# The 8x8 base of the triangular inverses: block doubling from size 1 on TensorE in place of substitution on VectorE

## The chip, the cores and the metric

One NeuronCore of a Trainium2 chip runs the whole program, in one launch. The metric is the device time of one execution in microseconds (us), from the first to the last instruction and what the runtime adds around them. Three runs of the kernel before took 4042.07, 4048.28 and 4054.17 us: a median of 4048.28.

## The reference

Two residual blocks follow each other on 512 tokens of 2048 channels, all in float32. The first has a gated convolution and a differential attention; the change doesn't touch it. The second mixes with two recurrences, each over a context of 256 tokens and then the 512 tokens themselves, in both directions. Both need inverses of unit lower triangular matrices:

```python
def gated_delta_chunked(q, k, v, beta, g, s0):       # chunks of 64 tokens, 8 heads of 128
    ...
    decay = jnp.exp(jnp.where(tril, g[..., :, None] - g[..., None, :], -jnp.inf))
    kb = k * beta[..., None]
    lmat = jnp.where(strict, jnp.einsum('bhncd,bhnsd->bhncs', kb, k) * decay, 0.0)
    tmat = lax.linalg.triangular_solve(eye + lmat, jnp.broadcast_to(eye, lmat.shape),
                                       left_side=True, lower=True, unit_diagonal=True)
    u = tmat @ (v * beta[..., None])
    wk = tmat @ (kb * jnp.exp(g)[..., None])
    ...
def rwkv7_scan(r, w, k, v, kk, b_vec, s0):           # 16 heads of 64, token by token
    def step(state, inp):
        sa = -jnp.einsum('bhvk,bhk->bhv', state, kk_t)
        state = (state * w_t[:, :, None, :] + sa[..., None] * b_t[:, :, None, :]
                 + v_t[..., None] * k_t[:, :, None, :])
        return state, jnp.einsum('bhvk,bhk->bhv', state, r_t)
```

The kernel works the second recurrence in chunks of 64 tokens too, and each chunk then needs the inverse of a unit triangular 64 x 64 matrix as well.

## The kernel before

**The engines.** Large products ("dense" below, L136 in `products`) take weights in blocks of 128 x 128 against 512 tokens (256 for the context), in three passes, since each float32 operand is cut into a high part (ScalarE, L104) and a rest (VectorE, L105, tile `wlo`). The recurrences add many small products on TensorE and elementwise work on VectorE and ScalarE.

**The order.** A scheduler orders each engine's instructions when the program is built, from priorities; every engine then works through its own list in order. Dense products that the recurrences don't wait for (the next heads' inputs, the output's products) stand between the recurrences' small ones, mostly in runs of six (`K.burst`).

**The inverse.** `inv64` (L337 to L405) gets in `nm` the matrices -M^T of `n` tiles, each with two 64 x 64 units on the halves of the partitions, and gives ((I + M)^-1)^T. First comes the base, the inverses of the 8 x 8 blocks on the diagonal, all on VectorE: a mask (L342) and a sum (L344) fetch the blocks, and substitution goes through the columns, six times the three instructions shuffle, product and sum (L351 to L353), each waiting for the one before. Four masked copies (L356) spread the result into 32 x 32 blocks (`iv_u`), and a transpose (L358) gives `iv_t`. Then come doubling levels, here two (8 to 16, 16 to 32): 4 products of 32 x 32 for each of the `n` tiles (L368), a copy by ScalarE (L370), again 4 `n` products (L374), a predicated copy that puts the new blocks into `iv_u` (L376), and a transpose (L377). A last step (L381 to L404) joins 32 to 64.

**How often.** `inv64` is called 56 times: by the gated delta rule (`gdn_core`, tiles `gd_*`) for 8 heads and 2 directions, with n = 2 for the context and n = 4 for the 512 tokens; by the second recurrence (`rwkv_pair`, tiles `rg_*`, two heads at a time) with n = 8, 8 times for the context and 16 times for the tokens. So n = 2, 4 and 8 come 16, 16 and 24 times. One float32 product of 32 x 32 leaves two records in the trace: a level's group of L368 or L374 has 8 n records, so 16, 32 and 64.

## Time and profile before

| | |
|---|---|
| median of 3 runs | 4048.28 us |
| the profiled execution, span | 4056.2 us |
| PE (TensorE products) busy | 3829.7 us, 94% |
| PEld (weight loads) busy | 2916.8 us, 72% |
| DVE (VectorE) busy | 2808.6 us, 69% |
| ACT (ScalarE) busy | 1389.2 us, 34% |
| POOL (GpSimd) busy | 479.8 us, 12% |
| mean granted TensorE clock | 0.964 |

The span goes from the first to the last instruction of the one execution that was profiled; of that execution no other time is given, and its span is 7.9 us above the median of the runs. Busy time is the time in which at least one instruction of the engine was under way; records of neighbouring products overlap, since they are pipelined. A granted clock of 1.00 is 2.4 GHz and 0.50 is 1.2 GHz; the mean of a stretch lies between.

The inverses stand in three stretches of the program: from 600 to 1700 us (the context, n = 2 and then 8, beside the first block's products), from 2400 to 3000 us (gated delta rule on the tokens, n = 4) and from 3000 to 3950 us (second recurrence, n = 8, at its start the last head's with n = 4).

### The profile page before, as it was taken

To read this page: it belongs to the slowest core of one execution; us is meant where nothing else is said; L and a number is where in the kernel's file an instruction comes from. 1 tells how busy PE (TensorE), PEld (TensorE's weight loads), DVE (VectorE), ACT (ScalarE), POOL (GpSimd) and SP (SyncE) were. 2 spreads that over 40 slices of the span, in tenths; PEclk is the share of its full clock that TensorE was granted. 3 is DMA by queue.
4 is the path that set the end of the run, shared out by engine and by line. 5 is a ranking of instruction groups with operands and counts; after the bars stand their busy time and mean duration, and the time that the engine had idled before them with its cause. 6 is when DMAs were issued, how large, how long until landed. Compare 5 with 4: busy or idle time off the path is not lost. (4 is left out here: it accounts for less than half of the span.)

```text
span 4056.2 us, 82730 instructions
## 1 busy us (share of the span) xinstructions
PE 3829.7 (94%) x33202; PEld 2916.8 (72%) x33202; DVE 2808.6 (69%) x7413; ACT 1389.2 (34%) x2825; POOL 479.8 (12%) x572
## 2 busy tenths in 40 slices
PE   8999878999999999999999799999999999999997
PEld 4676668876767767776887477877777777766776
DVE  3366787688777777744532977878667877777766
ACT  3312333323343434322322333333323443434333
POOL 0000221002110100000221301101001110111102
PEclk9999899999999999999999899999999998999998
DMA  8766435433334333424533332222223211222236
GB/s 320 266 212 200 157 127 165 146 113 110 126 114 125 104 104 99 149 91 143 207 113 122 104 96 69 71 72 74 81 84 107 67 64 55 76 67 88 91 120 203
DMA packets 213121, 497.01 MB, mean 123 GB/s; under 512 B 40576, under 2 KB 73600, under 8 KB 212736
## 3 DMA queue, kind: packets, MB, share of 16 engines
q1 hardware_dynamic: 212736, 491.72, 37.0%
q8 instruction: 261, 4.28, 0.4%
q14 instruction: 124, 1.02, 0.1%
HBM read 438.54 MB, written 53.08 MB: 121 GB/s over the span
## 5 line engine op out<-in xcount | busy, mean ns | idle before, releaser
L136 PE MATMUL pd<-big,whi 128*128 128x512 f32 x5344 | 1788.5, 412 | 9.1 <-ACT big L331 8.0
L136 PEld LDWEIGHTS pd<-big,whi 128*128 128x128 f32 x5344 | 965.7, 191 | 262.0 <-issue 27.8
L136 PE MATMUL pd<-big,wlo 128*128 128x512 f32 x2800 | 1114.0, 398 | 3.8 <-DVE wlo L105 3.8
L104 ACT CAST whi<-wraw 128x1024 fp32r<-128x1024 f32 (+2 forms) x500 | 506.7, 1014 | 1109.7 <-PE pd L136 1045.6
L105 DVE TENSOR_TENSOR wlo<-wraw,whi 128x1024 fp32r<-128x1024 f32 (+2 forms) x483 | 579.2, 1199 | 310.8 <-ACT whi L104 276.7
L136 PEld LDWEIGHTS pd<-big,wlo 128*128 128x128 f32 x2800 | 534.8, 191 | 128.0 <-DVE wlo L105 6.4
L136 PE MATMUL pd<-hc,whi 128*128 128x256 f32 x1184 | 236.3, 299 | 17.8 <-ACT gc_up L515 6.0
L136 PEld LDWEIGHTS pd<-hc,whi 128*128 128x128 f32 x1184 | 193.2, 200 | 23.4 <-ACT gc_up L515 6.4
L136 PE MATMUL pd<-hc,wlo 128*128 128x256 f32 x592 | 175.4, 297 | 28.3 <-DVE wlo L105 24.0
L136 PE MATMUL pd<-ext,whi 128*128 128x512 f32 x512 | 184.4, 401 | 3.8 <-DVE ext L105 3.8
L1075 DVE SCALAR_TENSOR_TENSOR cv_y<-cv_up,vec,cv_y 128x512 f32<-128x512 f32 x240 | 179.7, 749 | 4.7
L136 PE MATMUL pd<-fa,whi 128*128 128x512 f32 x448 | 153.1, 423 | 0.3 <-DVE wo L1462 0.2
L136 PEld LDWEIGHTS pd<-hc,wlo 128*128 128x128 f32 x592 | 117.9, 199 | 34.1 <-DVE wlo L105 27.8
L971 ACT ACTIVATE rg_zw<-rg_H,rg_wc 64x64 f32<-64x64 f32 x320 | 104.7, 343 | 47.1 <-DVE rg_H L989 38.7
L858 POOL TENSOR_TENSOR rg_bk<-rg_th,rg_L 64x512 f32<-64x512 f32 x48 | 67.7, 1410 | 425.5 <-ACT rg_L L837 193.0
L989 DVE SCALAR_TENSOR_TENSOR rg_H<-pc,rg_wc,rg_zw 64x64 f32<-64x64 f32 x320 | 90.5, 283 | 38.9 <-PE pc L981 30.5
L136 PEld LDWEIGHTS pd<-ext,whi 128*128 128x128 f32 x512 | 97.2, 190 | 27.8 <-DVE ext L105 4.6
L221 DVE SCALAR_TENSOR_TENSOR ada_ev<-wraw,cs_ada,ada_ev 128x512 f32<-128x512 f32 x120 | 94.8, 790 | 15.8 <-DMA wraw<-in_wada_dram 14.8
L520 DVE SCALAR_TENSOR_TENSOR gc_y<-gc_up,vec,gc_y 128x512 f32<-128x512 f32 (+1 forms) x160 | 103.2, 645 | 2.0
L136 PEld LDWEIGHTS pd<-fa,whi 128*128 128x128 f32 x448 | 82.2, 194 | 20.2 <-issue 1.1
L370 ACT COPY iv_y<-px 128x256 f32<-128x256 f32 (+2 forms) x112 | 33.0, 294 | 177.2 <-PE px L368 176.9
L906 PE MATMUL px<-rg_C,rg_bk 64*128 64x128 f32 x512 | 92.5, 311 | 0.3 <-DVE rg_C L909 0.3
(575 smaller groups left out, 5915.3 us busy)
## 6 DMA issues: line engine op xcount, KB each, us to landing
wraw<-in_w_dram SPq DMA_DIRECT2D x372, 512.0 KB, 3.6
wraw<-in_wada_dram SPq DMA_DIRECT2D x192, 512.0 KB, 4.6
wraw<-in_wo_dram SPq DMA_DIRECT2D x32, 512.0 KB, 3.5
sgl<-sgd SPq DMA_DIRECT2D x48, 256.0 KB, 3.4
wraw<-in_wout_dram SPq DMA_DIRECT2D x20, 512.0 KB, 4.1
wraw<-in_w_dram SPq DMA_DIRECT2D x32, 256.0 KB, 3.9
sgd<-msg SPq DMA_DIRECT2D x32, 256.0 KB, 3.7
wraw<-in_wco_dram SPq DMA_DIRECT2D x16, 512.0 KB, 3.5
```

Source lines behind the costliest of these rows:

```text
L104: K.nc.scalar.copy(hi, src)
L105: (eng or K.nc.vector).tensor_tensor(lo, src, hi.bitcast(F32), op=ALU.subtract)
L136: nc.tensor.matmul(ps[:, :T], lhsT=a[:, k], rhs=b, start=(n == 0), stop=(n == 3 * (k1 - k0) - 1))
L221: nc.vector.scalar_tensor_tensor(ev, raw[:, k], cs[:, kk, 0:1], ev, op0=ALU.mult, op1=ALU.add)
L370: nc.scalar.copy(ys, yp)
L520: nc.vector.scalar_tensor_tensor(y, up[:, t:t + T], w[:, t:t + 1], y, op0=ALU.mult, op1=ALU.add)
L858: nc.gpsimd.tensor_tensor(bk[uq, :, u], th[uq], F[uq], op=mul)
L906: nc.tensor.matmul(pg[:, m], lhsT=bk[q, 4 * r + m].rearrange("p x c -> p (x c)"), rhs=C[q, 4 * r + m, u], start=True, stop=True, tile_posi ...
L971: nc.scalar.activation(zw[hv[u], d], H[hv[u], ms[d], u], AF.Copy, scale=wn[hv[u], 4 * d + mn])
L989: nc.vector.scalar_tensor_tensor(Hn[hv[u], 4 * d + mn, u], pc3[hv[u], 2, d], wn[hv[u], 4 * d + mn], zw[hv[u], d], op0=mul, op1=ALU.add)
L1075: nc.vector.scalar_tensor_tensor(y, up[:, t:t + 512], w[:, t:t + 1], y, op0=ALU.mult, op1=ALU.add)
```

## The change

The 8 x 8 base goes. `iv_u` starts as the identity, written by ScalarE (L344 of the changed file), and two predicated copies put the entries of `nm` beside the diagonal into it, which is the inverse for blocks of 2 (one copy for each half of the partitions, as `nm` has its blocks at other columns there). From there the same doubling loop runs four levels, 2 to 4, 4 to 8, 8 to 16 and 16 to 32. The masks for the predicated copies grow from 2 to 6 for each direction; they are now read as integers straight from the constants, without the copy `cpi`.

```diff
-    ("ident", 128), ("ones", 128), ("bones", 128), ("m8", 64), ("i8", 8), ("m32", 4), ("m64", 2),
+    ("ident", 128), ("ones", 128), ("bones", 128), ("i32", 32), ("m64", 2),
...
-    ("cpm", 128),
+    ("cpm", 384),
...
-    cpi = K.const.tile([128, 128], I32, name="cpi")
-    nc.vector.tensor_copy(cpi, K.c["cpm"])
+    cpi = K.c["cpm"].bitcast(I32)
     for d in range(2):
-        for l in range(2):
-            K.cp[d, l] = cpi[:, 32 * (2 * d + l):32 * (2 * d + l) + 32]
+        for l in range(6):
+            K.cp[d, l] = cpi[:, 32 * (6 * d + l):32 * (6 * d + l) + 32]
...
-    nc.vector.tensor_tensor(tmp, nm, c["m8"].unsqueeze(1).to_broadcast([128, n, 64]), op=ALU.mult)
-    n8 = pool.tile([128, n, 8], F32, name="iv_n8")
-    nc.vector.tensor_reduce(n8, tmp.rearrange("p n (b e) -> p n e b", e=8), axis=AX.X, op=ALU.add)
-    u8 = pool.tile([128, n, 8], F32, name="iv_u8")
-    nc.vector.tensor_copy(u8, c["i8"].unsqueeze(1).to_broadcast([128, n, 8]))
-    sh = pool.tile([128, n, 8], F32, name="iv_sh")
-    i = 7 if d == 0 else 0
-    nc.vector.tensor_tensor(u8[:, :, i:i + 1], u8[:, :, i:i + 1], n8[:, :, i:i + 1], op=ALU.add)
-    for i in (range(6, 0, -1) if d == 0 else range(1, 7)):
-        nc.vector.stream_shuffle(sh, u8, [8 * (q // 8) + i for q in range(32)])
-        nc.vector.tensor_tensor(sh, sh, n8[:, :, i:i + 1].to_broadcast([128, n, 8]), op=ALU.mult)
-        nc.vector.tensor_tensor(u8, u8, sh, op=ALU.add)
     u32 = pool.tile([128, n, 32], F32, name="iv_u32")
-    for b in range(4):
-        nc.vector.tensor_scalar(u32[:, :, 8 * b:8 * b + 8], u8, c["m32"][:, b:b + 1], None, op0=ALU.mult)
     t32 = pool.tile([128, n, 32], F32, name="iv_t32")
+    nc.scalar.copy(u32, c["i32"].unsqueeze(1).to_broadcast([128, n, 32]))
+    for l in range(2):
+        nc.vector.copy_predicated(u32, K.cp[d, l].unsqueeze(1).to_broadcast([128, n, 32]), nm[:, :, 32 * l:32 * l + 32])
     nc.vector.transpose(t32.rearrange("p n e -> p (n e)"), u32.rearrange("p n e -> p (n e)"))
-    for lev in range(2):
+    for lev in range(2, 6):
...
-        for sz in (8,16):
+        for sz in (1,2,4,8,16):
             same=(q//(2*sz)==e//(2*sz)); jl=(q%(2*sz))<sz; il=(e%(2*sz))<sz
-            m.append(same&(jl&~il if d==0 else ~jl&il))
+            new=same&(jl&~il if d==0 else ~jl&il)
+            m+=[new&((p%64)//32==h) for h in range(2)] if sz==1 else [new]
```

The rest of the diff takes out comments and docstrings (so line numbers move by up to 11) and the argument `tmp` with its tile `iv_tmp`.

What this does to VectorE's list is seen in the first head of the gated delta rule on the context (n = 2). Before, the end of the base stands there: the last of the six rounds, the sum for the other direction's base, the masked copies and the transpose.

```order
L351 STREAM_SHUFFLE iv_sh<-iv_u_4785 128x16
L352 TENSOR_TENSOR iv_sh<-iv_sh,iv_n_4783 128x16
L353 TENSOR_TENSOR iv_u_4785<-iv_u_4785,iv_sh 128x16
L344 TENSOR_REDUCE iv_n_4910<-iv_tmp 128x16
L356 TENSOR_SCALAR iv_u_4807<-iv_u_4785,cst 128x2x8 x4
L105 TENSOR_TENSOR wlo<-wraw,whi 128x1024
L358 STREAM_TRANSPOSE iv_t_4812<-iv_u_4807 128x64
```

In the changed kernel the same place of VectorE's list has the second predicated copy from `nm` (here `gd_dd`), the transpose, and then already the end of the first added level, with other work between.

```order
L346 COPY_PREDICATED iv_u_4779<-cst,gd_dd 128x64
L615 TENSOR_TENSOR gd_dd<-gd_dd,TM_ctx 128x128
L347 STREAM_TRANSPOSE iv_t_4780<-iv_u_4779 128x64
L616 TENSOR_TENSOR gd_dd<-gd_dd,gd_kkd 128x128
L617 TENSOR_TENSOR gd_dx<-gd_dx,TM_ctx 64x128
L104 TENSOR_TENSOR wlo<-wraw,whi 128x1024
L618 TENSOR_TENSOR gd_dx<-gd_dx,gd_kkx 64x128
L720 SCALAR_TENSOR_TENSOR rm<-pd,vec,rm 96x255
L700 TENSOR_SCALAR rm_omu<-vec 128x1
L104 TENSOR_TENSOR wlo<-wraw,whi 128x1024
L365 COPY_PREDICATED iv_u_4779<-cst,px_4785 128x64
L366 STREAM_TRANSPOSE iv_t_4780<-iv_u_4779 128x64
```

The chain of 26 short instructions on VectorE is gone; three stay ahead of the first products.

On TensorE's list the place is the last inverse of the program (second recurrence, n = 8, so 32 products a group). Before, its first level is two groups with six dense products between them.

```order
L368 MATMUL px_39937<-iv_t_39935,rg_nr 32x32 x32
L136 MATMUL pd<-fa,whi 128x512 x2
L136 MATMUL pd<-fa,wlo 128x512
L136 MATMUL pd<-fa,whi 128x512 x2
L136 MATMUL pd<-fa,wlo 128x512
L374 MATMUL px_39937<-iv_u_39930,iv_y 32x32 x32
```

In the changed kernel the inverse's second level, one of the two that are new, stands at that place among products of the recurrence's own chain (`pc`, `po`).

```order
L357 MATMUL px_43546<-iv_t_43472,rg_nr 32x32 x32
L970 MATMUL pc<-rg_H,rg_bt 64x64 x4
L983 MATMUL po<-rg_nr,rg_H 64x64 x3
L363 MATMUL px_43546<-iv_u_43471,iv_y 32x32 x32
L983 MATMUL po<-rg_nr,rg_H 64x64
L938 MATMUL pc<-rg_H,rg_C 64x64 x4
L944 MATMUL po<-rg_C,rg_H 64x64 x4
L135 MATMUL pd<-fa,whi 128x512 x2
L135 MATMUL pd<-fa,wlo 128x512
```

Over the whole list the 22791 products become 27399, all of the difference in these groups, and the dense products, whose number stays, are cut into 977 runs instead of 874. The groups of the two levels stand in 249 pieces before and those of the four levels in 494 pieces after.

## Rows read from the trace of the kernel before

**Rows 1.** The page, busy time of each engine, share of the span, instructions.

```profile
PE 3829.7 (94%) x33202; PEld 2916.8 (72%) x33202; DVE 2808.6 (69%) x7413; ACT 1389.2 (34%) x2825; POOL 479.8 (12%) x572
```

**Rows 2.** Windows: PE, PEld, DVE, ACT, POOL busy, PE clock, DMA share, GB/s.

```profile
600.00:1700.00 1100.00, 1054.27 (x10046) 806.38 (x10046) 849.94 (x2548) 408.60 (x909) 114.44 (x158) 0.98 0.39 122
...
2400.00:3000.00 600.00, 592.48 (x5665) 470.92 (x5662) 463.13 (x1493) 186.42 (x362) 57.27 (x134) 0.99 0.23 74
3000.00:3950.00 950.00, 909.62 (x11540) 679.25 (x11540) 708.00 (x2050) 382.06 (x915) 113.78 (x101) 0.94 0.25 81
```

**Rows 3.** Waits of PE: us in total, times, longest us.

```profile
PE pd L136 <- DVE wlo L105: 27.9, 24, 3.6
...
PE px L368 <- DVE iv_u L346: 6.6, 8, 3.0
PE px L368 <- DVE iv_sh L352: 6.0, 8, 1.4
...
PE px L374 <- ACT iv_y L370: 0.9, 1, 0.9
```

**Rows 4.** Groups by line, DVE, the base: busy us, mean ns | idle before.

```profile
L352 DVE TENSOR_TENSOR iv_sh<-iv_sh,iv_n 128x64 f32<-128x64 f32 (+2 forms) x336 | 78.2, 233 | 7.0
L353 DVE TENSOR_TENSOR iv_u<-iv_u,iv_sh 128x64 f32<-128x64 f32 (+2 forms) x336 | 74.9, 223 | 7.1
...
L351 DVE STREAM_SHUFFLE iv_sh<-iv_u 128x64 f32<-128x64 f32 (+2 forms) x336 | 66.3, 197 | 0.6
...
L356 DVE TENSOR_SCALAR iv_u<-iv_u,cst 128x64 f32<-128x64 f32 (+2 forms) x224 | 40.6, 247 | 1.0
```

**Rows 5.** Groups by line, DVE and ACT, of the two doubling levels.

```profile
L377 DVE STREAM_TRANSPOSE iv_t<-iv_u 128x256 f32<-128x256 f32 (+2 forms) x112 | 38.6, 345 | 1.4
L376 DVE COPY_PREDICATED iv_u<-cpi,px 128x256 f32<-128x256 int32 (+2 forms) x112 | 38.1, 341 | 64.9 <-PE px L374 55.1 <-issue 7.1 <-ACT cz_th L1336 1.2
...
L370 ACT COPY iv_y<-px 128x256 f32<-128x256 f32 (+2 forms) x112 | 33.0, 294 | 177.2 <-PE px L368 176.9
```

**Rows 6.** Groups by line, PE, second half of the two levels.

```profile
L374 PE MATMUL px<-iv_u,iv_y 32*32 32x32 f32 x4608 | 65.0, 195 | 6.6 <-issue 5.7 <-ACT iv_y L370 0.9
```

**Rows 7.** Timeline of PE, n = 4: start us, us, instruction.

```profile
2415.54 0.39 PE L136 MATMUL pd<-big,wlo 128*128 128x512 f32 x1
...
2416.23 0.39 PE L136 MATMUL pd<-big,wlo 128*128 128x512 f32 x1
2416.55 0.45 PE L374 MATMUL px<-iv_u,iv_y 32*32 32x32 f32 x32
2416.93 0.73 PE L136 MATMUL pd<-big,whi 128*128 128x512 f32 x2
```

**Rows 8.** Timeline of PE, n = 8.

```profile
3905.07 0.40 PE L136 MATMUL pd<-fa,wlo 128*128 128x512 f32 x1
3905.39 0.75 PE L374 MATMUL px<-iv_u,iv_y 32*32 32x32 f32 x64
3906.08 0.74 PE L136 MATMUL pd<-fa,whi 128*128 128x512 f32 x2
```

**Rows 9.** Timeline of PE, n = 2.

```profile
830.17 0.39 PE L136 MATMUL pd<-big,wlo 128*128 128x512 f32 x1
830.49 0.33 PE L368 MATMUL px<-iv_t,gd_dd 32*32 32x32 f32 x16
830.75 0.73 PE L136 MATMUL pd<-big,whi 128*128 128x512 f32 x2
```

**Rows 10.** The chain that ended last: start us, us, what.

```profile
3950.43 38.32 PE pd L136 x168
```

**Rows 11.** Windows around one fall of the clock, columns as in rows 2.

```profile
3215.00:3218.40 3.40, 3.15 (x102) 2.86 (x88) 3.21 (x8) 1.83 (x4) 0.00 (x0) 1.00 0.31 105
3218.60:3222.00 3.40, 3.40 (x71) 2.44 (x70) 3.05 (x15) 0.31 (x1) 0.00 (x0) 0.50 0.53 192
```

More of the change, by code (lines that the diff above doesn't have):

```diff
@@ L333, in modulate_steps, with inv64 @@
         yield hi, lo
-def inv64(K, pool, upool, nm, n, d, px, tmp):
+def inv64(K, pool, upool, nm, n, d, px):
     nc = K.nc
     c = K.c
-    nc.vector.tensor_tensor(tmp, nm, c["m8"].unsqueeze(1).to_broadcast([128, n, 64]), op=ALU.mult)
-    n8 = pool.tile([128, n, 8], F32, name="iv_n8")
-    nc.vector.tensor_reduce(n8, tmp.rearrange("p n (b e) -> p n e b", e=8), axis=AX.X, op=ALU.add)
-    u8 = pool.tile([128, n, 8], F32, name="iv_u8")
-    nc.vector.tensor_copy(u8, c["i8"].unsqueeze(1).to_broadcast([128, n, 8]))
-    sh = pool.tile([128, n, 8], F32, name="iv_sh")
-    i = 7 if d == 0 else 0
-    nc.vector.tensor_tensor(u8[:, :, i:i + 1], u8[:, :, i:i + 1], n8[:, :, i:i + 1], op=ALU.add)
-    for i in (range(6, 0, -1) if d == 0 else range(1, 7)):
-        nc.vector.stream_shuffle(sh, u8, [8 * (q // 8) + i for q in range(32)])
-        nc.vector.tensor_tensor(sh, sh, n8[:, :, i:i + 1].to_broadcast([128, n, 8]), op=ALU.mult)
-        nc.vector.tensor_tensor(u8, u8, sh, op=ALU.add)
     u32 = pool.tile([128, n, 32], F32, name="iv_u32")
-    for b in range(4):
-        nc.vector.tensor_scalar(u32[:, :, 8 * b:8 * b + 8], u8, c["m32"][:, b:b + 1], None, op0=ALU.mult)
     t32 = pool.tile([128, n, 32], F32, name="iv_t32")
+    nc.scalar.copy(u32, c["i32"].unsqueeze(1).to_broadcast([128, n, 32]))
+    for l in range(2):
+        nc.vector.copy_predicated(u32, K.cp[d, l].unsqueeze(1).to_broadcast([128, n, 32]), nm[:, :, 32 * l:32 * l + 32])
     nc.vector.transpose(t32.rearrange("p n e -> p (n e)"), u32.rearrange("p n e -> p (n e)"))
-    for lev in range(2):
+    for lev in range(2, 6):
         ps = px()
@@ L629, in gdn_core @@
         nc.vector.tensor_tensor(dx[fq], dx[fq], kkx[fq], op=ALU.mult)
-        u64, u32, t32, ys = inv64(K, pool, pool, dd, nt, d, px[d], pool.tile([128, nt, 64], F32, name="iv_tmp"))
+        u64, u32, t32, ys = inv64(K, pool, pool, dd, nt, d, px[d])
         e0, z0 = (0, 32) if d == 0 else (32, 0)
@@ L917, in unit @@
                 nc.vector.tensor_tensor(C[hv[1 - u], :, u], pg[hv[1 - u]], bc(hv[1 - u], 64), op=mul)
-        u64 = inv64(K, prep, chn, nm, 8, 0, px, bk[:, :, 0])[0]
+        u64 = inv64(K, prep, chn, nm, 8, 0, px)[0]
         return wc, C, bt, ra, u64, H
@@ L1682, in cst @@
     c=np.arange(64)[None]
-    o['m8']=(c//8==(p%64)//8); o['i8']=(np.arange(8)[None]==p%8)
-    o['m32']=(np.arange(4)[None]==(p%32)//8); o['m64']=(np.arange(2)[None]==(p%64)//32)
+    o['i32']=(np.arange(32)[None]==p%32); o['m64']=(np.arange(2)[None]==(p%64)//32)
     o['ga0']=np.where(c>=p%64,0.0,-3e38); o['ga1']=np.where(c<=p%64,0.0,-3e38)
```

## The prediction, before the run

> **What bounds the kernel now.** I read the page first. PE is busy 94% of the span, VectorE 69% and ScalarE 34% [rows 1]. A busy share is a mean over stages, so I went on to the windows, cut where the inverses stand. In all three stretches PE is the fullest engine: 1054.3 of 1100 us, 592.5 of 600 and 909.6 of 950, against 849.9, 463.1 and 708.0 for VectorE [rows 2]. What PE has idle there is 45.7, 7.5 and 40.4 us, 93.6 in all. The third view was PE's waits. VectorE's base holds PE up a little: the first products of an inverse waited 6.6 and 6.0 us in total behind it, and dense products 27.9 us for `wlo`, which VectorE makes over the whole program [rows 3]. So some 40 us of waits for VectorE stand against a VectorE that the change makes lighter. The fourth view was the chain that ended last: after the last inverse PE still runs 168 dense products for 38.3 us without a break [rows 10]. Dense work is thus left when the recurrences are done. If the recurrences take longer, that work can move forward into their gaps; if PE gets more to do, the end moves.
>
> My reading: PE's own work sets the time, and what matters is how much PE time the new groups take out of the stream.
>
> **What the change adds on PE.** Two levels with two groups each, 4 groups a call: 64 groups with n = 2, 64 with n = 4, 96 with n = 8. What a group costs is read from the timeline where it stands in the dense stream. From one `wlo` product to the next are three dense products: 2416.23 - 2415.54 = 0.69 us, 0.23 each [rows 7]. With a group between them, two neighbouring dense products start 2416.93 - 2416.23 = 0.70 us apart for n = 4 [rows 7], 1.01 for n = 8 [rows 8] and 0.58 for n = 2 [rows 9]. Less the 0.23 that the dense product itself takes, a group standing alone costs 0.47, 0.78 and 0.35 us. That is the upper bound: 64 x 0.35 + 64 x 0.47 + 96 x 0.78 = 127 us. A group beside other small products doesn't pay the change from dense to small, 0.32 instead of 0.23; from its first product to the next start it takes 0.38, 0.69 and 0.26 in the same rows, which gives the lower bound of 64 x 0.26 + 64 x 0.38 + 96 x 0.69 = 107 us. The order says how many pay: the dense products are cut into 103 more runs, 103 x 0.09 = 9 us; and the 224 new groups stand in 245 pieces, 21 more ends at some 0.1 us (two pieces of 32 take 2 x 0.38 where one of 64 takes 0.69, two of 16 take 0.52 where one of 32 takes 0.38). I take 107 + 9 + 2 = **+118 us**. As a check, the second halves of the two present levels are busy for 65.0 us [rows 6], the first halves have the same number and shapes, and 2 x 65.0 = 130 counts tails that lie beside the next product.
>
> **What it does on VectorE and ScalarE.** At least 78.2 + 74.9 + 66.3 + 40.6 = 260 us of VectorE's work goes [rows 4]; the smaller groups of the base are on top. Two more levels add 38.6 + 38.1 us [rows 5], and the two copies from `nm` a call are as many again as the levels' predicated copies, some 38: a net of at least -145 us. It lies beside PE, and what it is worth is what PE waits for. Of the 12.6 us in front of the inverses most should go, since three VectorE instructions stand where 26 stood. The new levels bring their own waits: PE waited 0.9 us for ScalarE's copy and 5.7 us for issue in front of the present second halves [rows 3, 6], so as much again, 6.6. That is a net of **-6 us**. It could be -40 if all of `wlo`'s 27.9 and the 12.6 went, and +19 if the first level waited as before and every added level's first half as often as the base's 56 (12.6 for each 56, with some overlap gone, plus 6.6). I take -6, by the rows of the same handoffs. ScalarE gets 112 more copies at 294 ns, 33 us [rows 5], and 56 identity copies, at the same mean 16 us, beside 34% busy; I take zero, hidden by the dense products that the order puts between a level's halves. Without that cover PE would wait 0.29 us for each of the 112, 33 us. Queued behind such a copy is the cast that feeds dense weights (L104).
>
> **The clock.** In the third stretch, with the most small products, the granted clock is lowest, 0.94 against 0.98 and 0.99 [rows 2]; one fall from 1.00 to 0.50 came after 3.40 us in which PE was busy for 3.15 us with 102 records [rows 11]. The added 118 us run at about the mean of these stretches, 0.97, which costs 118 x 0.03 = **+4 us**. If more small products mean more falls, I allow 0.015 less in the first and third stretch, 2050 x 0.015 = 31 us; nothing, if they don't. The Trainium skill, "TensorE: Matmul & The Clock Gate", section on why this matters for your kernels, says that the clock is lost in idle gaps between bursts; by that rule a PE with more to do would lose less, and this term were zero or a small gain. Rows 11 don't fit it, as PE was not idle before that fall.
>
> The larger table of constants (1252 columns for 1040) and the missing copy `cpi` come once, at the start; no row here prices them, the load stands beside the first weights', and I take zero within 1 us either way.
>
> **The sum.** 118 - 6 + 4 = +116 us on the profiled 4056.2 us, a factor of 1.0286. That execution's span is 7.9 us above the median of the runs; 4048.28 x 1.0286 = **4164 us**. The bounds added up: 107 - 40 + 0 = +67 and 127 + 19 + 31 = +177, or 4115 to 4225.
>
> **The rivals.** *TensorE has room, and VectorE sets the pace (faster).* Weight loads are busy for only 72% of the span [rows 1], and VectorE for some three quarters of each stretch. If the small products slip into time that PE spends waiting for VectorE, they cost nothing and the 40 us of waits come back: 4016 us of span, 4008 on the median. The point from which it decides: where the idle time in front of PE is made by VectorE and is at least as long as the added products. The Trainium skill speaks for this, in "Perfetto Trace Analysis", section on identifying the most-contended engine: a busy share of matmuls misleads, as they are pipelined, and headroom is judged by the share of weight loads. Against it stand the rows of single groups, in which the next dense product starts later by the group's whole length [rows 7 to 9], so the room between weight loads isn't room for other products; and the named waits for VectorE's base are 12.6 us [rows 3]. Chance 0.07.
>
> *Half hidden.* The 93.6 us that PE idles in the three stretches takes up the new products, as independent work fits into waits of the chain. Then 118 - 94 = +24 us, 4072. For it: the recurrence's chain makes short waits on PE, and the order puts new groups among its products. Against: the order already had dense products to put there, and what idles now idles because something came later than planned. Chance 0.10.
>
> *The inverse's latency sets the end.* A round of the base is 197 + 233 + 223 ns, six are 3.9 us, and with the masked copies some 5 us [rows 4]. A new level is two groups of 0.75 us for n = 8, the copies and the transpose, 0.29 + 0.34 + 0.35, and twice six dense products of 0.23: some 5.2 us, two of them 10.4. If the units of the second recurrence follow one after the other, 16 x 5.4 = 86 us of delay arise in the third stretch; the dense products left at the end cover 38 [rows 10], and 48 us of new stalls come on top of the sum: 4212. For it: PE's order is fixed, and a late group holds up all behind it. Against: now there is dense work left over, so latency isn't what ends the program. Chance 0.15.
>
> That the groups don't come is excluded by the order.
>
> **How the numbers follow.** The forecast keeps 0.68. A measurement of this kernel tells about 0.3% from no change, 12 us. Faster by more than that takes nearly all of the first rival: 0.06. Within 0.3%: the rest of it and a part of the second, 0.05. Slower: 0.89. For 8 in 10 the range is 4100 to 4225: the sum's own bounds, all of the latency rival and the upper edge of the half-hidden one.
>
> **What would show it.** The 32 x 32 groups of the loop double in number with the same mean, some 65 us more busy time for each half; VectorE's busy time falls by 145 us or more; PE's share rises to 95% or 96% of a longer span. Dense products stay at 0.23 us. The growth is shared as the groups are: the 8 + 16 calls with n = 8 bring 96 x 0.69 to 0.78, about 70 us, two thirds of it in the recurrence on the tokens. Right by chance would be a longer span with no more than half of it in those groups; then waits for `iv_y` or `iv_u`, or a clock of 0.92 or less in the last third, must show. Wrong it is if the span grows by less than 60 us, above all if PE's idle time shrinks by as much as the groups add.

## The result, and the profile after

| | before | after |
|---|---|---|
| median | 4045.18 us (4 runs) | 4227.02 us (4 runs, 4216.30 to 4233.53) |
| profiled execution, span | 4056.2 us | 4214.5 us |
| mean granted clock, profiled execution | 0.964 | 0.964 |

The changed kernel is slower: ratio 1.0447, 95% interval 1.0424 to 1.0470. The 182 us between the medians stand against 116 us forecast, and 4227 us lies 2 us above the range. The profiled execution is the fastest of the four, and its granted clock (0.964) the highest; the others ran at 0.960, 0.960 and 0.963. That matters below: a second profile of the same kernel (experiment 4) has a span of 4237.1 us at 0.959, so two executions of one kernel differ by 23 us with their clock.

The page of the changed kernel, busy times, answers to [rows 1]:

```profile
PE 3985.6 (95%) x42418; PEld 3015.9 (72%) x42418; DVE 2628.6 (62%) x5956; ACT 1438.3 (34%) x2993; POOL 480.9 (11%) x572
```

VectorE lost 180 us, ScalarE gained 49, PE gained 156. The span grew by 158: nearly all of it is PE's busy time, and what PE idles stays about as it was (4056.2 - 3829.7 = 226.5 before, 4214.5 - 3985.6 = 228.9 after; 4237.1 - 4004.5 = 232.6 in experiment 4).

The same three stretches [rows 2], cut where the same work stands in the changed kernel:

```profile
600.00:1740.00 1140.00, 1097.98 (x13047) 822.85 (x13046) 764.07 (x1903) 424.37 (x975) 116.47 (x160) 0.98 0.37 116
2455.00:3084.00 629.00, 627.41 (x7697) 488.47 (x7695) 412.52 (x1089) 199.40 (x407) 58.85 (x138) 1.00 0.24 72
3084.00:4100.00 1016.00, 963.19 (x15659) 726.16 (x15658) 652.09 (x1619) 396.10 (x962) 113.61 (x99) 0.94 0.24 74
```

They are longer by 40, 29 and 66 us, 135 of the 158. In the second PE idles 2 us of 629: there is nothing left to hide anything in. In the third it idles 53 us instead of 40, at the lowest clock.

PE's waits (us in total, times, longest) answer to [rows 3]:

```profile
PE pd L135 <- DVE wlo L104: 20.3, 19, 3.6
...
PE px L357 <- DVE iv_t L366: 9.9, 7, 4.2
...
PE px L363 <- issue: 7.7, 9, 1.5
...
PE px L380 <- DVE iv_t L366: 5.0, 2, 4.7
...
PE px L363 <- ACT iv_y L359: 3.7, 7, 1.1
```

The waits for the base (12.6 us) are gone and those for `wlo` fell by 7.6. In their place PE waits for the transposes and copies between the levels.

The groups by line, VectorE's and ScalarE's part of the levels and PE's second halves [rows 5, 6], and the new start of an inverse (L344):

```profile
L363 PE MATMUL px<-iv_u,iv_y 32*32 32x32 f32 x9216 | 131.6, 196 | 11.4 <-issue 7.7 <-ACT iv_y L359 3.7
...
L366 DVE STREAM_TRANSPOSE iv_t<-iv_u 128x256 f32<-128x256 f32 (+2 forms) x224 | 77.4, 346 | 4.4
L365 DVE COPY_PREDICATED iv_u<-cst,px 128x256 f32<-128x256 int32 (+2 forms) x224 | 76.4, 341 | 196.2 <-PE px L363 161.5 <-issue 25.1 <-ACT rg_H L931 2.8
L359 ACT COPY iv_y<-px 128x256 f32<-128x256 f32 (+2 forms) x224 | 65.8, 294 | 328.9 <-PE px L357 328.2
...
L344 ACT COPY iv_u<-cst 128x256 f32<-128x256 f32 (+2 forms) x56 | 18.3, 327 | 32.6 <-PE px L389 22.1 <-PE px L628 9.8 <-PE px L477 0.2
```

Everything doubled in number at the old mean: 65.0 us of the second halves became 131.6, at 196 ns a record for 195.

PE's timeline (start, us, instruction; in brackets the idle time before it) in the second recurrence on the tokens, a group between dense products [rows 8], and ahead of it a place where a level came late:

```profile
4008.91 0.40 PE L135 MATMUL pd<-fa,wlo 128*128 128x512 f32 x1
4013.51 1.07 PE L357 MATMUL px<-iv_t,rg_nr 32*32 32x32 f32 x64 [4.20 <-DVE iv_t L366]
...
4017.16 1.22 PE L135 MATMUL pd<-fa,whi 128*128 128x512 f32 x2
...
4021.80 0.75 PE L363 MATMUL px<-iv_u,iv_y 32*32 32x32 f32 x64
4022.49 0.73 PE L135 MATMUL pd<-fa,whi 128*128 128x512 f32 x2
4023.05 0.40 PE L135 MATMUL pd<-fa,wlo 128*128 128x512 f32 x1
4023.29 0.62 PE L135 MATMUL pd<-fa,whi 128*128 128x512 f32 x2
4023.75 0.40 PE L135 MATMUL pd<-fa,wlo 128*128 128x512 f32 x1
...
4055.91 0.39 PE L135 MATMUL pd<-fa,wlo 128*128 128x512 f32 x1
4056.23 0.75 PE L363 MATMUL px<-iv_u,iv_y 32*32 32x32 f32 x64
4056.91 0.73 PE L135 MATMUL pd<-fa,whi 128*128 128x512 f32 x2
```

The last three rows repeat the price: 4056.91 - 4055.91 = 1.00 us from one dense product to the next with a group of 64 between them, 1.01 in the forecast. The rows from 4021.80 to 4023.75 show a price that the forecast left out. The pair of dense products right behind the group takes 4023.05 - 4022.49 = 0.56 us to the next start, the following pair 4023.75 - 4023.29 = 0.46: a group costs some 0.10 us behind it too, beside the 0.09 in front of it that the forecast had. The first rows show another. PE waits 4.20 us for a transpose, and then a group takes 1.07 us instead of 0.75 and a pair of dense products 1.22 instead of 0.73. The windows over the wait, the stretch behind it and the one after that show the granted clock (the third figure from the end, as in [rows 2]):

```profile
4009.40:4013.40 4.00, 0.00 (x0) 0.00 (x0) 3.97 (x8) 0.00 (x0) 0.41 (x1) 0.92 0.28 79
4013.60:4019.00 5.40, 5.40 (x144) 4.57 (x145) 3.10 (x6) 2.30 (x4) 0.00 (x0) 0.50 0.52 179
4021.00:4025.00 4.00, 3.74 (x109) 2.98 (x108) 2.77 (x6) 0.37 (x1) 0.00 (x0) 1.00 0.00 0
```

It is at 0.50, the lower of its two levels (1.2 GHz), for the work behind the wait, and back at 1.00 two us later.

The chain that ended last [rows 10], start, us, what:

```profile
4106.06 53.32 PE pd L135 x234
```

After the last inverse there are now 234 dense products in a row for 53 us, where there were 168 for 38: the recurrences got longer, and still dense work was left over.

**Where the 182 us are.** Three sums are used in the table of the experiments. *Own slots*: for each matmul of the inserted groups the time from its start to the next matmul's start, added up over a profile, less the same of before. *The clock's part*: (1 - mean clock) x time, since a stretch at half clock loses half its time; taken from the medians of a kernel's runs, less the same of before. (Slots that fell into slow stretches are a little longer for that too, so the two overlap by some us.) *The rest* is what is left. A step of 0.001 of clock is 4 us, so the rest is good to some 10 us.

For the changed kernel in experiment 4 (five runs): 177 us over before, of which the clock's part is 0.040 x 4232 - 0.035 x 4055 = 27 us, own slots 138 us (17 of them waits of more than 1 us in front of a group, so 120 of work), and the rest 12 us. A wait that moved from another place to a group counts in these own slots in full, so they don't say what PE waits more.

A second account, of the profiled executions, leaves no rest. The time from each product's start to the next product's start is split into PE's idle time, half of the time that PE worked at half clock, and what remains, the product's slot at full clock. Against the profile before (4056.2 us), in us, rounded:

| | inserted groups | dense products | other products | PE idle | half clock | span |
|---|---|---|---|---|---|---|
| the changed kernel, first profile | +109 | +23 | +24 | +2 | 0 | +158 |
| 4 the changed kernel again | +108 | +23 | +21 | +6 | +22 | +181 |
| 2 base kept, levels in the chain | +105 | +22 | +16 | +53 | +33 | +228 |
| 3 base kept, levels' results unread | +110 | +18 | +23 | +28 | +33 | +213 |
| 9 small products alone | +107 | +14 | +19 | +46 | +58 | +244 |
| 10 large products alone | +100 | +18 | +2 | +8 | +7 | +135 |
| 11 before, runs of 12 | +1 | -16 | +16 | +19 | +3 | +24 |
| 13 changed, large products added | +182 | +34 | +27 | -3 | -15 | +225 |
| 14 changed, runs of 3 | +104 | +43 | +17 | +8 | +61 | +233 |

The changed kernel's own part is in the first two rows: the groups cost 108 us, the products that were there before get 44 to 47 us dearer at full clock, PE idles 2 to 6 us more, and the clock makes the difference between the two executions.

### The profile page after: what moved, and what is told of

Same layout as the page of the kernel before. It is cut to its first block, busy times and chain, and to the rows that moved or that the text cites. A ratio compares the mean times of both kernels' runs of the same rounds, so it can differ in the third digit from the quotient of the medians.

```text
span 4214.5 us, 100154 instructions
## 1 busy us (share of the span) xinstructions
PE 3985.6 (95%) x42418; PEld 3015.9 (72%) x42418; DVE 2628.6 (62%) x5956; ACT 1438.3 (34%) x2993; POOL 480.9 (11%) x572
## 5 line engine op out<-in xcount | busy, mean ns | idle before, releaser
L365 DVE COPY_PREDICATED iv_u<-cst,px 128x256 f32<-128x256 int32 (+2 forms) x224 | 76.4, 341 | 196.2 <-PE px L363 161.5
L359 ACT COPY iv_y<-px 128x256 f32<-128x256 f32 (+2 forms) x224 | 65.8, 294 | 328.9 <-PE px L357 328.2
L363 PEld LDWEIGHTS px<-iv_u,iv_y 32*32 32x32 f32 x9216 | 102.7, 107 | 79.1 <-issue 51.6
L363 PE MATMUL px<-iv_u,iv_y 32*32 32x32 f32 x9216 | 131.6, 196 | 11.4 <-issue 7.7
```

The lines of the kernel that those rows point to most:

```text
L359: nc.scalar.copy(ys, yp)
L363: nc.tensor.matmul(zp[q, m], lhsT=ys[q, m], rhs=u32[q, m], start=True, stop=True, tile_position=(32 * r, 32 * r))
L365: nc.vector.copy_predicated(u32, K.cp[d, lev].unsqueeze(1).to_broadcast([128, n, 32]), zp)
```

## The experiments

The theory after the result: PE's own time sets the pace, so the groups cost their slots, and something on top, either the clock that small products lower or the latency of the levels' handoffs. Each kernel was timed against the kernel before on the same chip; what they gave stands together here (medians; clock is the median over the runs).

| | ratio [95%] | us over before | clock | clock's part | own slots | rest |
|---|---|---|---|---|---|---|
| 1 base out, two levels | 1.000 [0.998, 1.002] | -3 | 0.963 | +8 | 0 | -11 |
| 2 base kept, levels in the chain | 1.058 [1.055, 1.060] | +234 | 0.953 | +60 | 128 | +46 |
| 3 base kept, levels' results unread | 1.053 [1.050, 1.056] | +215 | 0.9575 | +40 | 135 | +40 |
| 4 the changed kernel again | 1.044 [1.041, 1.047] | +177 | 0.960 | +27 | 138 | +12 |
| 5 large products for the levels | 1.076 [1.074, 1.078] | +305 | 0.963 | +23 | 217 | +65 |
| 6 three levels | 1.019 [1.017, 1.021] | +76 | 0.9645 | +9 | 59 | +8 |
| 7 change for n = 8 alone | 1.030 [1.027, 1.032] | +118 | 0.962 | +21 | 84 | +13 |
| 8 base of 16, one level | 1.019 [1.018, 1.021] | +80 | 0.9455 | +87 | -63 | +56 |
| 9 small products alone | 1.062 [1.060, 1.065] | +254 | 0.948 | +82 | 124 | +48 |
| 10 large products alone | 1.036 [1.034, 1.039] | +151 | 0.9615 | +20 | 106 | +25 |
| 11 before, runs of 12 | 1.007 [1.006, 1.009] | +31 | 0.961 | +21 | 0 | +10 |
| 12 changed, runs of 12 | 1.036 [1.034, 1.038] | +146 | 0.963 | +18 | 129 | -1 |
| 13 changed, large products added | 1.060 [1.058, 1.063] | +241 | 0.966 | +8 | 194 | +39 |
| 14 changed, runs of 3 | 1.057 [1.053, 1.061] | +226 | 0.9545 | +57 | 132 | +37 |
| 15 changed, runs of 9 | 1.041 [1.039, 1.044] | +168 | 0.9605 | +29 | 128 | +11 |

**1. The base goes, nothing comes.** The changed kernel without levels 2 to 4 and 4 to 8.

```diff
-    for lev in range(2, 6):
+    for lev in range(4, 6):
```

> The changed kernel with only the two levels that were there before (8 to 16, 16 to 32); the 2-to-4 and 4-to-8 levels are left out, so the 8 x 8 blocks aren't inverted. It has VectorE's base gone and nothing added on TensorE. Theory P (TensorE's own time is what the change costs): within 0.4% of the kernel before, a ratio of 0.993 to 1.000, as VectorE's relief returns at most the waits of some 6 to 40 us. Theory L (the latency of the inverses sets the end): the chain of an inverse is some 5 us shorter than before, and the ratio falls to 0.98 or less. Theory O (the new order or the missing base costs by itself, for example by worse mixing): a ratio above 1.005.

```profile
PE 3825.1 (95%) x33202; PEld 2915.5 (72%) x33202; DVE 2555.9 (63%) x5732; ACT 1404.9 (35%) x2881; POOL 488.6 (12%) x572
```

Its inverses are not right, as the 8 x 8 blocks aren't inverted; the rest of the work is the same. VectorE is 253 us lighter than before, PE does the same work and idles 221.8 us instead of 226.5, and the time is the same to 0.2%. So the base cost nothing while it stood there, and VectorE doesn't set the pace.

**2 and 3. The levels come, the base stays.** First in the inverse's chain with an empty mask, then with their results in tiles that nobody reads.

```diff
-    for lev in range(2):
+    for lev in (2, 2, 0, 1):          # 2: a mask of zeros (both kernels)
...
+        if lev == 2:                  # kernel 3 only
+            nc.vector.tensor_copy(x32, zp)
+            nc.vector.transpose(w32..., x32...)
+            continue
```

> The kernel before, with its base on VectorE, and two more levels of the loop ahead of the two that are there; their predicated copy has an empty mask, so they change nothing in the result but stand in the chain of each inverse. Theory P: the two levels cost what they cost in the changed kernel, a ratio of 1.035 to 1.05, and VectorE's extra load doesn't show. Theory L: the chain of an inverse grows by 10 us instead of 5, so clearly more than the changed kernel, 1.06 or more. Theory O: less than the changed kernel, 1.03 or below.

> As the kernel with two more levels in the chain, but what they give goes to tiles that nothing reads, so the two levels that count needn't wait for them; TensorE, ScalarE and VectorE do the same work. Theory P: the same time as with the levels in the chain, within 0.7%. Theory L: at least 1.5% less than with the levels in the chain.

Kernel 3 doesn't take the levels out of the chain as far as its expectation has it. A level's products go to `px`, which has one buffer under each of its two names, so the next level waits until VectorE has copied that buffer out, here into the unread tile:

```profile
PE px L370 <- DVE iv_x L379: 3.7, 6, 1.1
```

What it spares the next level is the transpose. The two kernels lie 19 us apart, with intervals that touch. By the medians that is the clock's part (60 and 40 us); in the two profiled executions, with clocks of 0.955 and 0.956, PE idles 25 us more in kernel 2. So this pair doesn't tell what an inverse's latency costs, and kernel 2 at 1.058 lies between the ranges of its theories (up to 1.05, and 1.06 or more). What does tell for the changed kernel is that PE idles only 2 to 6 us more in it than before. Both kernels are 38 to 57 us dearer than the changed one, though the base by itself is worth nothing (experiment 1): PE idles 53 and 28 us more than before. Whether VectorE's load or the longer inverse does that, they don't show.

**4. The changed kernel again**, unchanged, beside the same runs of the kernel before as 1 to 3.

> The changed kernel again, beside the same runs of the kernel before as the other three: 1.040 to 1.048 by every theory. Its runs say how far the profiled execution (158 us longer than the one of before) stands from the median (182 us).

Its profile, with the clock at 0.959, is nearer to the median than the first.

```profile
PE 4004.5 (95%) x42418; PEld 3030.6 (72%) x42418; DVE 2631.5 (62%) x5956; ACT 1438.1 (34%) x2993; POOL 481.7 (11%) x572
```

**5. As much time in large products.** The kernel before with 280 large float32 products (128 x 512, unread), 3, 4 or 7 behind an inverse.

```diff
+    for _ in range({2: 3, 4: 4, 8: 7}[n]):
+        ps = px()
+        nc.tensor.matmul(ps, lhsT=c["ident"], rhs=c["all_cst"][:, 0:512], start=True, stop=True)
```

> The kernel before with 3, 4 or 7 more large float32 products (128 x 128 weights, 512 columns, results unused) in each inverse with n = 2, 4 or 8: 280 in all, by the 0.43 us from start to start of such products in the trace of before some 120 us, about what the new groups take on TensorE in the changed kernel. Theory C (a third of the unforeseen time is the clock, because the added work is small products): TensorE's time rises by as much, but the time at half clock stays at about 300 us or falls, and the ratio is 1.024 to 1.034. Theory D (any longer program, or any more work on TensorE, runs more at half clock and with more stalls): half clock for 340 us or more as in the changed kernel, a ratio of 1.038 or more.

The groups by line show why the time missed what I expected:

```profile
L381 PE MATMUL px<-cst 128*128 128x512 f32 x560 | 304.4, 626 | 1.6 <-DVE iv_u L377 1.6
```

A float32 product leaves two records, 560 for 280, and I had paid for one: 217 us of slots instead of 120. The run still says that PE work whose results nobody reads delays the end by its slots and 30% more (the rest is 65 us), and that 217 us of large products take less clock (23 us) than 124 us of small ones in experiment 9 (82).

**6 and 7. Parts of the change.** One added level instead of two; and both levels, but in the second recurrence (n = 8) alone.

```diff
-    for lev in range(2, 6):
+    for lev in range(3, 6):           # kernel 6
...
+    if n == 8:                        # kernel 7: the new start and range(2, 6), else the old base and two levels
```

> The changed kernel without the 2-to-4 level (so the 4 x 4 blocks are wrong): one added level instead of two. If each level costs its groups, its waits and its share of the clock: half of the changed kernel's 4.4%, 1.019 to 1.025. If the waits or the clock set in only beyond a point: 1.016 or less for one level and the rest with the second. If one more level already fills what was free: 1.028 or more.

> The change for the second recurrence alone (n = 8), the gated delta rule keeps VectorE's base. By the prices of the groups 66 to 75 of the 118 us are here; if the unforeseen part is spread as the groups are, 1.025 to 1.028. If clock and waits come from the second recurrence alone: 1.031 to 1.036. If they come from the gated delta rule: 1.018 to 1.021.

The first added level costs 1.9%, the second 2.5% more: no level is free, so PE has no room for them. The 96 groups with n = 8 cost 118 of the 177 us, 67%; by the forecast's prices they are 66 to 75 of 118, 56 to 64%. So 1.030 lies between the expectation for an even spread (up to 1.028) and the one in which clock and waits come from the second recurrence alone (from 1.031).

**8. The other way: a base of 16.** 14 rounds on VectorE, one level instead of two.

```diff
-    for i in (range(6, 0, -1) if d == 0 else range(1, 7)):
+    for i in (range(14, 0, -1) if d == 0 else range(1, 15)):
...
-    for lev in range(2):
+    for lev in (1,):
```

> The other way: the kernel before with a 16 x 16 base by substitution on VectorE (14 rounds instead of 6) and one doubling level instead of two. If TensorE's small groups cost as in the change, 60 to 65 us of groups and some 15 us of clock go: 0.980 to 0.986. If VectorE's 8 more rounds, 3 x 8 x 56 instructions at 0.22 to 0.3 us, some 300 to 400 us, come up in TensorE's waits: 0.995 or more.

63 us of slots went from PE, and the kernel got slower by 80 us. The window over the second recurrence on the tokens (columns as in [rows 2]):

```profile
3111.00:4028.00 917.00, 835.79 (x8799) 621.30 (x8799) 749.49 (x2351) 344.87 (x836) 105.30 (x90) 0.89 0.23 77
```

Here it is VectorE's latency that tells: PE idles 81 of 917 us there, where the kernel before has 37 of 846 (its row stands under experiments 9 and 10), and the clock is at 0.89. The clock's part (87 us) is more than the whole loss. Against the base of 8, a base of 2 takes 1.044, one of 4 (experiment 6, where its own making is left out) 1.019, and one of 16 takes 1.019: more for PE and more for VectorE both lose.

**9 and 10. Bare products.** The kernel before, with 224 groups of 32 x 32 products, two behind each level's predicated copy; and with 136 large float32 products at the same places. Nothing reads the results. But the groups take the one buffer of `px` in turn with the levels: each waits for the predicated copy ahead of it, and the next level waits for the groups.

```diff
+        for _ in range(2):                        # kernel 9
+            ps = px()
+            ...
+                    nc.tensor.matmul(xp[q, m], lhsT=nm[q, m, 0:32], rhs=ys[q, m], start=True, stop=True,
+                                     tile_position=(32 * r, 32 * r))
...
+        for _ in range({2: 1, 4: 1, 8: 2}[n] if lev else {2: 1, 4: 1, 8: 1}[n]):     # kernel 10
+            ps = px()
+            nc.tensor.matmul(ps, lhsT=c["ident"], rhs=c["all_cst"][:, 0:512], start=True, stop=True)
```

> The kernel before with the 224 groups that the change adds, same sizes and tiles, but as bare work on TensorE: their results are unused, and no copy, predicated copy or transpose belongs to them. What the changed kernel adds was taken apart in its second profile into 115 us of products at full clock, 32 us of waits and 35 us of half clock. Theory C (the clock falls because of the small products themselves): 115 us and a large part of the 35, a ratio of 1.033 to 1.038, with the time at half clock at 330 us or more. Theory W (clock and waits both come from the handoffs between TensorE, ScalarE and VectorE): 115 us alone, 1.026 to 1.030, with half clock at about 300 us.

> The kernel before with 136 unused large float32 products at the same places of the inverses, about the same time on TensorE as the 224 groups: each leaves two records, and the 280 of the earlier run took 217 us from start to start, so 136 take 106 us. Theory C: no more half clock than before, about 300 us or less, and a ratio of 1.024 to 1.030, below the small products alone. If any unused work at these places makes waits, as the earlier run's 75 us of stalls for 217 us of products say: up to 1.037.

The windows over the second recurrence on the tokens, first with small products:

```profile
3220.00:4185.00 965.00, 897.40 (x14823) 671.08 (x14823) 647.63 (x1876) 344.00 (x842) 105.64 (x90) 0.90 0.21 67
```

and with large ones:

```profile
3165.00:4075.00 910.00, 862.66 (x10843) 622.83 (x10843) 658.62 (x1880) 344.40 (x844) 107.89 (x90) 0.93 0.23 71
```

In the kernel before, the same stretch has

```profile
3089.00:3935.00 846.00, 808.90 (x10732) 600.86 (x10731) 647.76 (x1879) 344.21 (x840) 105.92 (x90) 0.93 0.24 75
```

Kernel 9 missed both of its theories by far (1.062, where neither had more than 1.038); kernel 10, at 1.036, lies inside what it had for unread work that makes waits (up to 1.037). With slots of nearly the same length (124 and 106 us) the small products cost 103 us more than the large ones, and 62 of these are the clock's part. That is a large cost in clock for small products that nobody reads, but not one without waits: over the whole program PE idles 46 us more than before with the small products and 8 with the large ones, and in the stretch shown it has 29 waits of over 1 us, 51 us, against 17 with 40 us. Theory W, by which products without handoffs cost their slots alone, is not tested here, since the groups have the handoff over `px`.

**11 and 12. Longer runs of dense products.** `K.burst` from 6 to 12 for the second recurrence on the tokens, in both kernels.

```diff
-        K.burst = 6
+        K.burst = 12
```

> The kernel before with the large products in runs of 12 instead of 6 in the second recurrence on the tokens; same work, dense products in 806 runs instead of 874. Theory B (changing between large and small products is what costs): 68 breaks less at 0.09 us, 6 us, a ratio of 0.997 to 1.000. Theory C (the clock falls in stretches without large products, here longer ones): more half clock, 320 us or more, and a ratio above 1.003.

> The same in the changed kernel: 906 runs of dense products instead of 977. Theory B: 6 to 10 us less than the changed kernel, a ratio to the kernel before of 1.040 to 1.043. Theory C: its half clock grows above 350 us and it is slower than the changed kernel, 1.047 or more.

The kernel before gets slower by 0.7%, the changed one faster by 38 us against experiment 4, and its clock in that stretch is up:

```profile
3205.00:4118.00 913.00, 889.18 (x14966) 687.87 (x14965) 591.84 (x1470) 365.86 (x894) 106.78 (x89) 0.95 0.27 83
```

The first number is what theory C expected (above 1.003, with 320 us or more at half clock; the trace has 322). The second is what neither expected: it is below B's 1.040, and C had it slower. The stretch now holds 1572 dense products instead of 1369, so two things changed at once: how many stand there, and how long their runs are.

**13 to 15. Which of the two.** Three theories: the clock goes by the share of full-size products (A), by the small groups wherever they stand (B), or by the length of the dense runs (C). Kernel 13 adds one large float32 product behind each level of the inverses with n = 8 to the changed kernel; 14 and 15 set the runs to 3 and 9.

```diff
+        if n == 8:                                # kernel 13
+            pw = px()
+            nc.tensor.matmul(pw, lhsT=c["ident"], rhs=c["all_cst"][:, 0:512], start=True, stop=True)
...
-        K.burst = 6
+        K.burst = 3                               # kernel 14; 9 in kernel 15
```

> The changed kernel with 96 large float32 products more (128x512 against the identity, two records of about 0.39 us each, results unread), one behind each of the four levels of the 24 inverses with n = 8. Theory A, the clock in the second recurrence on the tokens goes by how many full-size products stand in it for each microsecond: 64 of the 96 lie there, so 1392 + 128 = 1520 records in some 970 us, 1.57 a us instead of 1.49; time at half clock there falls from 160 to about 130 us, mean clock of the runs 0.962 or more; 4232 + 75 - 15 = 4292 us, ratio 1.060. Theory B, the small groups cost clock wherever they stand, whatever is beside them: half time there stays at 150 us or more, mean clock 0.960, 4232 + 75 = 4307 us or more, ratio 1.064. Theory C, the length of the runs of dense products sets it: as B, since the runs stay at six.

> The changed kernel with dense products in runs of 3 instead of 6 in the second recurrence on the tokens: by the order 1371 dense products there instead of 1377, in 315 runs instead of 213. Theory A (number of full-size products for each microsecond): half time there stays at about 160 us, clock 0.959 to 0.960; 102 more breaks x 0.09 = 9 us, 4241 us, ratio 1.046. Theory B (the small groups themselves): the same. Theory C (length of the runs): half time there 190 us or more, mean clock 0.955 or less, 4232 + 9 + 20 = 4260 us or more, ratio 1.052 or more.

> The changed kernel with runs of 9 instead of 6 there: by the order 1365 dense products in that stretch, as many as with 6, in 176 runs instead of 213, and 366 instead of 387 behind it. Theory A: half time there stays at about 155 us, clock 0.960, 37 fewer breaks x 0.09 = 3 us, 4229 us, ratio 1.043. Theory B: the same. Theory C: half time there falls about as far as with runs of 12 (96 us), mean clock 0.963, some 30 us less, 4200 us, ratio 1.037.

The windows over the same stretch, with runs of 3:

```profile
3175.00:4150.00 975.00, 927.17 (x14779) 673.75 (x14779) 597.43 (x1460) 357.97 (x885) 105.61 (x90) 0.87 0.20 63
```

with runs of 6, the changed kernel of experiment 4 and the same kernel in its first profile:

```profile
3186.00:4110.00 924.00, 872.79 (x14781) 655.62 (x14780) 593.97 (x1454) 357.11 (x885) 106.01 (x90) 0.91 0.22 68
```

```profile
3180.00:4088.00 908.00, 858.87 (x14786) 645.25 (x14786) 592.89 (x1455) 356.60 (x884) 106.10 (x90) 0.93 0.22 69
```

with runs of 9:

```profile
3187.00:4094.00 907.00, 860.72 (x14782) 653.69 (x14780) 599.88 (x1468) 360.23 (x888) 106.89 (x90) 0.92 0.23 70
```

with runs of 6 and the large products added:

```profile
3191.00:4158.00 967.00, 917.82 (x14933) 660.73 (x14932) 604.36 (x1457) 359.64 (x886) 109.57 (x90) 0.95 0.21 65
```

Runs of 3, 6 and 9 do the same work (14779 to 14786 products) and differ in the order alone. Between 3 and 6 the difference is clear: 0.87 against 0.91 and 0.93, and a time ratio of 1.057 against 1.044, with intervals apart. So small groups don't cost a fixed amount of clock (B falls), and neither does the share of large products alone set it (A had 1.046 for runs of 3); the order counts, as C has it. Between 6 and 9 nothing is clear: 0.92 lies between the two profiles of the kernel with 6, the medians of the clock are 0.960 and 0.9605, the intervals of the ratios overlap, and C's 1.037 lies outside the one measured (1.0387 to 1.0435), A's 1.043 inside. In kernel 13 the runs stayed at six and the clock rose to 0.95 (median over the runs 0.966 instead of 0.960), with the time 57 us up for 85 us more of slots, which is A's number (4292 forecast, 4289 measured). PE idles about as long there as without the added products, 49 and 51 us in the stretch, so fewer waits are not the reason. Share and order both act; none of the three theories holds for all three runs.

The traces' records of the clock show more than the mean. A fall is here a time at 0.50 between two at 1.00; in the second recurrence on the tokens there are

| | falls | mean length, us | PE idle in the stretch, us |
|---|---|---|---|
| before | 18 | 6.4 | 37 |
| changed, first profile | 19 | 6.1 | 49 |
| changed, experiment 4 | 19 | 8.4 | 51 |
| 8 base of 16 | 15 | 13.4 | 81 |
| 9 small products alone | 21 | 8.9 | 68 |
| 10 large products alone | 21 | 6.2 | 47 |
| 12 changed, runs of 12 | 16 | 6.0 | 24 |
| 13 changed, large products added | 19 | 4.9 | 49 |
| 14 changed, runs of 3 | 16 | 15.6 | 48 |
| 15 changed, runs of 9 | 21 | 6.7 | 46 |

The clock falls about as often in all of them. What differs is how long it stays down, and that doesn't follow PE's idle time: with 46 to 51 us of it the mean length is 4.9, 6.1, 6.2, 6.7, 8.4 or 15.6 us.

## Why the prediction was right and wrong

**The direction and the cause were right.** PE's own time sets the pace, and the new groups take it. Removing VectorE's 253 us is worth nothing (experiment 1), and PE's idle time did not shrink. "TensorE has room" would have given 4008 us; what it rested on, weight loads at 72%, is at 72% after as well, with 4608 more records in each half of the levels. "Half hidden" falls with experiment 6: one level costs 76 us for 59 us of slots.

**The price of the groups was right, that of the breaks is the step that failed.** The +118 was 107 for the groups from their first product to the next start, 9 for 103 more breaks and 2 for split groups. At full clock the groups measure 108 and 109. But the products that were there before got 44 and 47 us dearer, where the forecast had 11. Two things in it were wrong, and both are told here as breaks. A break of the dense stream was priced in front of the group alone, 0.32 for 0.23, but the dense products behind it are slower too, in the kernel before already; these rows stand on either side of the group in [rows 7]:

```profile
2415.76 0.63 PE L136 MATMUL pd<-big,whi 128*128 128x512 f32 x2
...
2417.50 0.39 PE L136 MATMUL pd<-big,wlo 128*128 128x512 f32 x1
```

The pair inside the run takes 2416.23 - 2415.76 = 0.47 us to the next start, the pair behind the group 2417.50 - 2416.93 = 0.57. So the 0.47, 0.78 and 0.35 us of a single group were not the upper bound that the text calls them. With both ends a break is some 0.2 us, and the profiles bear it out: the dense products got 23 us dearer with 103 more runs here, 43 us with 204 more runs in experiment 14, and 16 us cheaper with 69 fewer in experiment 11. And the recurrences' own small products, which got 21 and 24 us dearer, were put at nothing, since a group beside other small products was said not to pay a change. By the traces the groups stand in 491 pieces instead of 249, many of them beside such products; that these are the reason is likely, but no run separates it. Groups and breaks together are 152 us, above their bound of 127, while PE's idle time and the clock stayed inside theirs.

**The single group and the shares.** A group between dense products stands at 1.00 us for 1.01 forecast. The groups with n = 8 have 67% of the cost for 56 to 64% by their prices (experiment 7).

**Latency sets the end: the number was near, the mechanism wrong.** Its 4212 us lies 15 us from the result. But its point of decision, that the dense work left at the end is used up, did not come: 234 products were left instead of 168. And the 48 us of new stalls did not come either: PE idles 2 and 6 us more in the two profiles. The nearness was luck.

**The waits were off by little.** I had -6 us, from waits for VectorE that go (12.6) and waits of the levels that come (6.6). PE's idle time rose by 2 and 6 us, inside the bounds of -40 and +19. In experiment 1 all those waits could go, and PE's idle time fell by 5 us. What the rows of the two present levels didn't show is where waits would stand: 17 us of long ones now lie in front of the groups, as the wait of 4.20 us does, and about as much has gone from other places.

**The clock was mis-sized.** I had +4 us, from the mean clock of the stretches, with +31 as the bound if small products meant more falls. Measured are +27 by the runs' medians, +22 in the profile of experiment 4, and nothing in the first profile, which is the fastest run: this term moves by as much between executions of one kernel. More falls did not come (18 before, 19 and 19 after in the last stretch); what there is of it lies in their length (6.4 us before, 6.1 and 8.4 after). I saw a row that pointed to small products (a fall after a stretch in which PE was busy, [rows 11]) and took no price from it. In the changed kernel of experiment 4, 8 of the 19 falls came after 10 us in which PE idled less than 0.1 us; in experiment 8 PE idled 0.96 us or more in the 10 us before each of the 15, and at 4013 us the clock is low after 4.20 us of waiting. The Trainium skill, "TensorE: Matmul & The Clock Gate", section on why this matters for your kernels, ties the loss to idle gaps between bursts. The place at 4013 us agrees with that and experiment 8 fits it; the 8 falls without idle time go beyond it.

With 108 for the groups, 44 for the breaks, 6 of idle time and 22 of clock the sum is 180, for 181 between the profile before and that of experiment 4. The forecast had 107, 11, -6 and 4: of the 64 us that it lacks, the breaks are 33, the clock 18 and the idle time 12.

**What stays open.** What exactly sets how long the clock stays low among small products (share, order or short waits) is not separated. Nor why PE idles 28 to 53 us more once the levels come with the base kept (experiments 2 and 3) and 46 us more with unread small products (experiment 9), but only 2 to 6 in the changed kernel; the shared buffer of `px` is one candidate for experiment 9, and a run with a buffer of their own for the unread groups would test it. And the kernel before loses by runs of 12 (21 of its 31 us are the clock's part), where the changed one gains; I don't know why. No version run here beats the kernel before.

## What to carry to other kernels

Where PE is busy 95% of the time, work moved to it costs its full slots, however free another engine becomes, and breaks the stream around it, at some 0.2 us for each more run of dense products here; count the breaks at both ends. Test first what the relieved engine's work is worth by leaving it out. Price small products by the clock too: write the time lost to it, (1 - mean clock) x time, beside every run, since in ten of these fifteen kernels its change was larger than the rest. And where an order mixes dense products with small ones, the length of the dense runs has to be tuned again after the mix changes (runs of 12 cost the kernel before 31 us and saved the changed one 38).

## What the runs showed of the hardware

- The granted clock also fell where PE was hardly idle among small products of 32 x 32: in the changed kernel's second recurrence on the tokens 8 of 19 falls came after 10 us with less than 0.1 us of idle time.
- Between kernels the falls in that stretch differ little in number (15 to 21) and much in length (4.9 to 15.6 us in the mean).
- At equal work the order alone moved the clock of that stretch: 0.87 with dense runs of 3, 0.91 and 0.93 with runs of 6, worth 42 us of the whole time between the medians.
- A group of 32 x 32 products between dense ones costs time at both ends: a dense product takes 0.32 us instead of 0.23 in front of it, and the pair behind it 0.56 instead of 0.46. The dense products got dearer with the number of their runs, 23 us for 103 more and 43 us for 204 more.
- One float32 product of 128 x 512 leaves two records, some 0.39 us a slot (217 us for 560 records).
- The time follows the mean clock from run to run of one and the same kernel: single runs of the kernel before took 4038.7 us at 0.970 and 4071.2 us at 0.960.
